# A two-layer decoder kernel: 68 products that nobody reads ahead of blocks of feed-forward products, and a new order

## The chip, the cores and the metric

One Trainium2 chip, one core of it. A time is the device time of one execution of the whole program in microseconds (us); a kernel's time is the median of its timed executions. The engines of the core run side by side, each through its own instructions in order: TensorE (PE) for matrix products, VectorE (DVE) and ScalarE (ACT) for elementwise work, GpSimd (POOL), and SyncE (SP), which issues the loads and stores (DMA).

## The reference

A decoder trunk of two layers on 256 positions of 1024 channels. Layer 0 is a gated linear recurrence and a SwiGLU feed-forward stage; then one key/value projection is made of its output; layer 1 is causal attention over these keys and a second feed-forward stage; a norm ends it. Each stage is modulated by the conditioning vector `c`.

```python
def swiglu(h, w_gate, w_up, w_down):
    return (jax.nn.silu(h @ w_gate) * (h @ w_up)) @ w_down

    for l in range(DEPTH):
        if l == N_A_LAYERS:
            kv_mod = cs @ kv_mod_w + kv_mod_b
            kv = shared_kv(x, kv_mod[:, :D], kv_mod[:, D:], kv_norm, w_kv)
        ...
        h = modulate(rmsnorm(x, norm_mix[l]), sh_m, sc_m)
        ...
        x = x + g_m[:, None, :] * mix
        h = modulate(rmsnorm(x, norm_ffn[l]), sh_f, sc_f)
        x = x + g_f[:, None, :] * swiglu(h, ffn_w_gate[l], ffn_w_up[l], ffn_w_down[l])
    return rmsnorm(x, final_norm)
```

`D_FF` is 2816, all data are float32.

## The kernel before

The stream of activations is kept transposed, as eight tiles of 128 channels by 256 positions. Weights come from memory in units of 128 partitions by up to 2048 columns (`raw_`, loaded by SP). ACT rounds each unit to the fp32r format (`whi_`, line 439), DVE takes the rest (`wlo_`, line 440), and one float32 product is made of three fp32r products (`mm3`, lines 387 to 389): high weights by high activations, high by low, low by high. Each is 128x128 weights by 256 columns. Some products are made in plain fp32 instead (line 449 and the sums of squares); such a product shows as two records.

The two feed-forward stages are f0 and f1 (the function `ffn`). In each, `f_st` are sums of squares over channels (products with a matrix of ones), `f_g` the products of the first 256 hidden channels with the activations not yet normed (`f_u`), so that they can start ahead of the norm, `f_p` those of the others (blocks i = 1 to 10, gate and up, q = 0 and 1), and `f_d` the products back to 1024 channels, eight of two halves with eleven weight tiles each. Behind f0 come the sums `n_st`, the keys `kp` (again with activations not yet normed, `kv_u`), the relative positions `rp` and the values `vp`; the attention ends in `ao`, with the weights `wo`. The residuals (line 611) give the next stream (`f0x`, `x3`), ACT squares it (`n_sq`, `f_sq`) and DVE adds the squares (line 539). The columns of modulation (`sc_`, `sh_`, `g_`) are made on DVE from rows loaded by DMA (line 462).

No loop of the chip sets the order. The program is recorded as operations with a cost in microseconds, reads and writes, and a planner in Python lays them out for each engine: of the operations that are ready, the one of the smallest rank goes first, where the rank is the place in the program plus a number from the table `PRIO`, by engine and kind of tile. Tiles are taken from pools of slots (four of `whi`, four of `wlo`, four of `raw`, eight of PSUM, among others), so an operation that writes a slot waits for the last reader of what lay there.

## Time and profile before

| what | us |
|---|---|
| median of two timed executions | 614.14 (612.71 to 615.57) |
| the profiled execution | 608.61 |
| its span, first to last instruction | 606.8 |
| PE busy in it | 585.9 |
| DVE busy | 471.8 |
| ACT busy | 340.6 |

A row of the profile's timeline is one instruction or a run of like ones on one engine: its start, how long it took, its engine, its line of the kernel, what it writes and reads. PE's products are pipelined: a duration reaches into the next product, so what a product costs is read from one start to the next. In brackets stands how long the engine idled ahead of it and what it waited for.

### The profile page before, as it was taken

Reading aid. Unit: us, or ns where it says so; the run is one execution under the profiler, and the core shown is the slowest. Engines: PE = TensorE matmul, PEld = TensorE weight load, DVE = VectorE, ACT = ScalarE, POOL = GpSimd, SP = SyncE. Lnnn points to the kernel's source line nnn. Section 1 sums busy time; section 2 is a strip of 40 time slices with the busy share of each in tenths; the row PEclk is TensorE's granted clock in tenths of the full one; section 3 lists DMA queues with packets and bytes.
Section 4 is the critical chain, followed back from the end, with each engine's and each line's share of the span. In section 5 each row is a group of like instructions: output and inputs, shape, how many; then the busy total and the mean of one; then the engine's idle time right before and its main releaser. Section 6 shows DMA issues by size and latency. Waiting matters only on the chain.

```text
span 606.8 us, 11423 instructions
## 1 busy us (share of the span) xinstructions
PE 585.9 (97%) x4706; PEld 563.2 (93%) x4706; DVE 471.8 (78%) x743; ACT 340.6 (56%) x509; POOL 1.2 (0%) x10
## 2 busy tenths in 40 slices
PE   3999989999999999999999999998999999999996
PEld 1999868998999999999999889998999999999996
DVE  6998788977997898788878969889997654545542
ACT  6537898718653443343336899747664444434432
POOL 0000000000000000000000000000000000000000
...
GB/s 307 353 339 239 332 355 355 278 383 224 350 312 323 336 348 323 257 334 315 377 295 357 203 143 322 282 332 245 218 306 274 214 203 165 144 144 192 191 1 70
DMA packets 33362, 162.94 MB, mean 269 GB/s; under 512 B 3700, under 2 KB 4893, under 8 KB 23966
## 3 DMA queue, kind: packets, MB, share of 16 engines
...
## 4 chain that ended last, share of the span: by engine, by line
PE 63%; DMA 18%; DVE 12%; ACT 3%; issue 3%; SPq 0%; DVEq 0%; ACTq 0%
PE ps_f_p L388 11%; PE ps_f_p L387 11%; PE ps_f_p L389 11%; PE ps_f_d L388 3%; PE ps_f_d L389 3%; PE ps_f_d L387 3%; PE ps_ga L449 3%; DMA mraw_mr_sh_kv_m__2730<-in_kvmod 2%; DVE wlo_f0c_l L440 2%; DMA raw_sh_f_r<-in_modp 1%; DMA mraw_mr_g_m_m__3469<-in_mod 1%; DMA raw_wix<-in_win_x 1%; PE ps_qp L389 1%; PE ps_qp L388 1%; PE ps_qp L387 1%
## 5 line engine op out<-in xcount | busy, mean ns | idle before, releaser
L388 PE MATMUL ps_f_p<-t_f_l,whi_f0b_h 128*128 128x256 f32 x320 | 89.7, 280 | 0.0
L387 PE MATMUL ps_f_p<-t_f_h,whi_f0b_h 128*128 128x256 f32 x320 | 89.5, 280 | 0.0
L389 PE MATMUL ps_f_p<-t_f_h,wlo_f0b_l 128*128 128x256 f32 x320 | 89.3, 279 | 0.0
L389 PE MATMUL ps_f_p<-t_f_h,wlo_f1b_l 128*128 128x256 f32 x320 | 88.5, 276 | 0.0
L387 PE MATMUL ps_f_p<-t_f_h,whi_f1b_h 128*128 128x256 f32 x320 | 88.4, 276 | 0.0
L388 PE MATMUL ps_f_p<-t_f_l,whi_f1b_h 128*128 128x256 f32 x320 | 88.4, 276 | 0.0
L388 PEld LDWEIGHTS ps_f_p<-t_f_l,whi_f0b_h 128*128 128x128 f32 x320 | 60.1, 188 | 0.2 <-DVE t_f_l L568 0.2
L387 PEld LDWEIGHTS ps_f_p<-t_f_h,whi_f0b_h 128*128 128x128 f32 x320 | 60.2, 188 | 0.0
L389 PEld LDWEIGHTS ps_f_p<-t_f_h,wlo_f1b_l 128*128 128x128 f32 x320 | 60.1, 188 | 0.1
L388 PEld LDWEIGHTS ps_f_p<-t_f_l,whi_f1b_h 128*128 128x128 f32 x320 | 60.1, 188 | 0.0
L387 PEld LDWEIGHTS ps_f_p<-t_f_h,whi_f1b_h 128*128 128x128 f32 x320 | 60.1, 188 | 0.0
L389 PEld LDWEIGHTS ps_f_p<-t_f_h,wlo_f0b_l 128*128 128x128 f32 x320 | 59.8, 187 | 0.0
L440 DVE TENSOR_TENSOR wlo_f1b_l<-raw_f1b_r,whi_f1b_h 128x2048 fp32r<-128x2048 f32 x20 | 45.6, 2289 | 18.1 <-ACT whi_f1b_h L439 18.1
L439 ACT ACTIVATE whi_f1b_h<-raw_f1b_r 128x2048 fp32r<-128x2048 f32 x20 | 38.2, 1912 | 24.8 <-issue 11.9
L439 ACT ACTIVATE whi_f0b_h<-raw_f0b_r 128x2048 fp32r<-128x2048 f32 x20 | 38.2, 1910 | 21.5 <-issue 19.1
L388 PE MATMUL ps_f_d<-t_f_al,whi_f0c_h 128*128 128x256 f32 x176 | 49.2, 280 | 0.8 <-DVE t_f_al L607 0.8
L389 PE MATMUL ps_f_d<-t_f_ah,wlo_f0c_l 128*128 128x256 f32 x176 | 49.3, 280 | 0.0
L387 PE MATMUL ps_f_d<-t_f_ah,whi_f0c_h 128*128 128x256 f32 x176 | 49.1, 279 | 0.0
L440 DVE TENSOR_TENSOR wlo_f0b_l<-raw_f0b_r,whi_f0b_h 128x2048 fp32r<-128x2048 f32 x20 | 45.6, 2287 | 4.2 <-ACT whi_f0b_h L439 4.1
L389 PE MATMUL ps_f_d<-t_f_ah,wlo_f1c_l 128*128 128x256 f32 x176 | 48.6, 276 | 0.0
L387 PE MATMUL ps_f_d<-t_f_ah,whi_f1c_h 128*128 128x256 f32 x176 | 48.6, 276 | 0.0
L388 PE MATMUL ps_f_d<-t_f_al,whi_f1c_h 128*128 128x256 f32 x176 | 48.6, 276 | 0.0
(469 smaller groups left out, 1661.3 us busy)
## 6 DMA issues: line engine op xcount, KB each, us to landing
...
```

The lines of the kernel that those rows point to most:

```text
L387: nc.tensor.matmul(o, h_, a_, start=start, stop=False, skip_group_check=skip)
L388: nc.tensor.matmul(o, h_, b_, start=False, stop=False, skip_group_check=skip)
L389: nc.tensor.matmul(o, l_, a_, start=False, stop=stop, skip_group_check=skip)
L439: act(n - o, lambda: nc.scalar.activation(hi.ap[:, o:n], raw.ap[:, o:n], AF.Copy), (raw,), (hi,))
L440: tt(n - o, lambda: nc.vector.tensor_sub(lo.ap[:, o:n], raw.ap[:, o:n], hi.f[:, o:n]), (raw, hi), (lo,))
L449: pe(n * 0.0016875 + 0.002, lambda: nc.tensor.matmul(ps.ap[:, c:c + n], lo.ap[:, o:o + w], xh.ap[:, xo:xo + n], start=start, stop=stop, sk ...
```

## The change

Two things. First, ahead of 68 blocks of fp32r products in f0 and f1 one product more is issued. The blocks are the first of each eight in `f_p` with j = 0 (i from 2 to 10, q = 0 and 1) and the first of each eleven in `f_d`. The kinds are taken in turn from a list of 24: eighteen are fp32r with 2 to 512 columns, which read the high weights that the next product reads and the first activations; six are fp32 with 2 to 128 columns, a matrix of ones by the identity. All write one PSUM tile of the stage, `f0_side` or `f1_side`, which nothing reads. A block with such a lead asks for the whole tile of activations in place of one half of it. Second, all numbers in `PRIO` are others, so that all engines' orders change. The results are the same.

```diff
 PRIO = {
     "PE": {
-        "cps": -877, "n_st": -1, "xb": 779, "yb": 1804, "ga": -19, "sh_f_ps": -1801, "sh_f_pt": 1118, "wo": -42,
...
+        "n_st": 1947, "xb": 1797, "yb": -17, "ga": -541, "sh_f_ps": 91, "sh_f_pt": 840, "wo": 1008, "g_m_ps": -28,
...
-        def mm3(cost, out, wh, wl, xh, xl, start, stop, R, Wr, skip=False):
+        def mm3(cost, out, wh, wl, xh, xl, start, stop, R, Wr, skip=False, pre=None):
             def fn():
+                if pre is not None:
+                    pre()
                 o = out()
...
+        ahead = [(1, 2), (1, 34), (1, 64), (1, 98), (1, 130), (1, 160), (1, 194), (1, 226), (1, 250), (1, 258), (1, 260),
+                 (1, 262), (1, 266), (1, 272), (1, 288), (1, 320), (1, 384), (1, 512), (0, 2), (0, 16), (0, 33), (0, 64),
+                 (0, 97), (0, 128)]
+        turn_of = [0]
+        side = {}
+
+        def gemm(out, key, wu, o, xu, start, stop, skip=False, w=P, n=S, cost=0.3275, lead=False):
...
+            pre, R, Wr = None, (hi, lo) + ((xh, xl) if n > S or lead else ((xh, xo), (xl, xo))), ((ps, key),)
+            if lead:
+                two, m = ahead[turn_of[0] % len(ahead)]
+                turn_of[0] += 1
+                d = side["ps"]
+                Wr += ((d, 0),)
+                if two:
+                    pre = lambda: nc.tensor.matmul(d.ap[:, :m], hi.ap[:, o:o + w], xh.ap[:, :m], start=True, stop=True)
+                else:
+                    R += (ident, ones)
+                    pre = lambda: nc.tensor.matmul(d.ap[:, :m], ones.ap, ident.ap[:, :m], start=True, stop=True)
+                cost += max(0.1, m * (0.00046 if two else 0.0017))
...
+            side["ps"] = PS(f"{name}_side")
...
-                                gemm((pq[q], j * S), 0, wq[q], (j * KC + k) * P, hx(h, k), k == 0, k == KC - 1)
+                                gemm((pq[q], j * S), 0, wq[q], (j * KC + k) * P, hx(h, k), k == 0, k == KC - 1,
+                                     lead=(j == 0 and k == 0))
...
-                        gemm((ps, 0), 0, wu, kk * P, hx(aa, k), k == 0, k == FT - 1)
+                        gemm((ps, 0), 0, wu, kk * P, hx(aa, k), k == 0, k == FT - 1, lead=(kk == 0))
```

The lines of the changed kernel are numbered 2 to 20 higher: its `mm3` has lines 389 to 391, the conversions are 441 and 442, the squares' sums 559, the residuals 631, the leads 469 (fp32r) and 472 (fp32).

In the new order of PE a lead stands like this inside f0, here of 272 columns; the block that it opens has the weights `f0b81`:

```order
L389 MATMUL ps_f0_p71_2503<-t2_f0_h2_1732,whi_f0b71_h_2406 128x256
L390 MATMUL ps_f0_p71_2503<-t2_f0_l2_1776,whi_f0b71_h_2406 128x256
L391 MATMUL ps_f0_p71_2503<-t2_f0_h2_1732,wlo_f0b71_l_2431 128x256
L469 MATMUL ps_f0_side_1848<-t2_f0_h0_1664,whi_f0b81_h_2534 128x272
L389 MATMUL ps_f0_p81_2649<-t2_f0_h0_1664,whi_f0b81_h_2534 128x256
L390 MATMUL ps_f0_p81_2649<-t2_f0_l0_1675,whi_f0b81_h_2534 128x256
L391 MATMUL ps_f0_p81_2649<-t2_f0_h0_1664,wlo_f0b81_l_2570 128x256
```

It stands directly ahead of the first product of its block and takes the same weights `whi_f0b81_h`.

PE where f0 ends, before. `f0_d7` is the last block of f0, `kp` the keys, `n2_st` the sums:

```order
L389 MATMUL ps_f0_d7_3652<-t2_f0_ah10_3059,wlo_f0c71_l_3585 128x256
L387 MATMUL ps_kp0_3717<-t1_kv_u1_h_3746,whi_wk0_h_3614 128x258
L388 MATMUL ps_kp0_3717<-t1_kv_u1_l_3006,whi_wk0_h_3614 128x258
...
L389 MATMUL ps_kp2_3735<-t1_kv_u2_h_3749,wlo_wk0_l_3636 128x258
L544 MATMUL ps_n2_st_3806<-t1_n2_sq0_3767,ones_132 128x256
...
L544 MATMUL ps_n2_st_3806<-t1_n2_sq7_3808,ones_132 128x256
L387 MATMUL ps_kp3_3742<-t1_kv_u2_h_3749,whi_wk0_h_3614 128x258
```

and after:

```order
L391 MATMUL ps_f0_d7_3637<-t2_f0_ah10_3075,wlo_f0c71_l_3609 128x256
L564 MATMUL ps_n2_st_3796<-t1_n2_sq0_3765,ones_132 128x256
...
L564 MATMUL ps_n2_st_3796<-t1_n2_sq7_3789,ones_132 128x256
L389 MATMUL ps_kp0_3818<-t1_kv_u0_h_2725,whi_wk0_h_3635 128x258
L390 MATMUL ps_kp0_3818<-t1_kv_u0_l_3806,whi_wk0_h_3635 128x258
```

Key products stood behind the last `f_d` and ahead of the sums, and now the sums come first and all key products behind them.

DVE at the same place, before. `f0x_7` is the residual that the last `f_d` gives, `kv_u1_l` the low part of an input of the keys:

```order
L440 TENSOR_TENSOR wlo_wv0_l_3721<-raw_wv0_r_3612,whi_wv0_h_3700 128x2048
L601 SCALAR_TENSOR_TENSOR t1_kv_u1_l_3006<-t1_f0x_1_3236,sc_kv_m_158,t1_kv_u1_h_3746 128x256
...
L611 SCALAR_TENSOR_TENSOR t1_f0x_7_3765<-ps_f0_d7_3652,g_f0_m_157,t1_x1_7_1580 128x256
L539 TENSOR_TENSOR t1_n2_sq0_3767<-t1_n2_sq0_3767,t1_n2_sq1_3769 128x256
...
L539 TENSOR_TENSOR t1_n2_sq0_3767<-t1_n2_sq0_3767,t1_n2_sq3_3773 128x256
L440 TENSOR_TENSOR wlo_wv4_l_3802<-raw_wv4_r_3644,whi_wv4_h_3777 128x2048
```

and after:

```order
L631 SCALAR_TENSOR_TENSOR t1_f0x_7_3763<-ps_f0_d7_3637,g_f0_m_157,t1_x1_7_1591 128x256
L559 TENSOR_TENSOR t1_n2_sq0_3765<-t1_n2_sq0_3765,t1_n2_sq1_3767 128x256
L482 SCALAR_TENSOR_TENSOR mraw_mr_g_m1_m__3734,g_m1_m_168<-mraw_mr_g_m1_m__3734,csb_130 128x1024
L559 TENSOR_TENSOR t1_n2_sq0_3765<-t1_n2_sq0_3765,t1_n2_sq2_3769 128x256
...
L442 TENSOR_TENSOR wlo_wv0_l_3787<-raw_wv0_r_3679,whi_wv0_h_3727 128x2048
L559 TENSOR_TENSOR t1_n2_sq0_3765<-t1_n2_sq0_3765,t1_n2_sq3_3771 128x256
L442 TENSOR_TENSOR wlo_wv4_l_3794<-raw_wv4_r_3751,whi_wv4_h_3784 128x2048
...
L621 SCALAR_TENSOR_TENSOR t1_kv_u0_l_3806<-t1_f0x_0_3148,sc_kv_m_158,t1_kv_u0_h_2725 128x256
```

The low parts for the keys stood ahead of the last residual, and now they stand behind it, behind all sums of squares, a column of modulation (`g_m1`) and two conversions of weights.

DVE where the attention hands over to f1, before. `x3_` are the residuals of the attention, `f1_u0_l` the first low part for f1's `f_g`:

```order
L539 TENSOR_TENSOR t1_f1_sq0_4806<-t1_f1_sq0_4806,t1_f1_sq2_4825 128x256
L582 TENSOR_TENSOR f1_sl_194<-sh_f1_m_170,f1_sh_193 128x8
...
L539 TENSOR_TENSOR t1_f1_sq0_4806<-t1_f1_sq0_4806,t1_f1_sq3_4832 128x256
...
L601 SCALAR_TENSOR_TENSOR t1_f1_u0_l_4859<-t1_x3_0_4797,sc_f1_m_169,t1_f1_u0_h_4813 128x256
...
L601 SCALAR_TENSOR_TENSOR t1_f1_u1_l_4864<-t1_x3_1_4804,sc_f1_m_169,t1_f1_u1_h_4845 128x256
```

and after:

```order
L631 SCALAR_TENSOR_TENSOR t1_x3_7_4892<-ps_ao3_4638,g_m1_m_168,t1_f0x_7_3763 128x256
...
L559 TENSOR_TENSOR t1_f1_sq0_4839<-t1_f1_sq0_4839,t1_f1_sq3_4894 128x256
L442 TENSOR_TENSOR wlo_f1b11_l_4906<-raw_f1b11_r_4678,whi_f1b11_h_4883 128x2048
L533 TENSOR_TENSOR sh_f1_m_170<-sh_f1_m_170,vec_129 128x8
...
L482 SCALAR_TENSOR_TENSOR mraw_mr_g_f1_m__4815,g_f1_m_191<-mraw_mr_g_f1_m__4815,csb_130 128x1024
L602 TENSOR_TENSOR f1_sl_194<-sh_f1_m_170,f1_sh_193 128x8
L621 SCALAR_TENSOR_TENSOR t1_f1_u0_l_4932<-t1_x3_0_4827,sc_f1_m_169,t1_f1_u0_h_4920 128x256
```

Between the last sum of squares and `f1_u0_l` a conversion of weights (`f1b11`) and a modulation column (`g_f1`) have come in, and the column `sh_f1` is finished later.

## Rows read from the trace of the kernel before

**Rows 1.** The page: busy shares, and one of the costliest groups.
```profile
PE 585.9 (97%) x4706; PEld 563.2 (93%) x4706; DVE 471.8 (78%) x743; ACT 340.6 (56%) x509; POOL 1.2 (0%) x10
...
L388 PE MATMUL ps_f_p<-t_f_l,whi_f0b_h 128*128 128x256 f32 x320 | 89.7, 280 | 0.0
```

**Rows 2.** Waits of PE, the first and the last of seven: us in total, times, longest.
```profile
PE ps_xb L677 <- ACT t_h L563: 4.7, 2, 4.4
...
PE ps_f_d L388 <- DVE t_f_al L607: 0.8, 1, 0.8
```

**Rows 3.** PE's timeline from f0 to the keys.
```profile
330.91 0.39 PE L388 MATMUL ps_kp<-t_kv_u_l,whi_wk_h 128*128 128x258 f32 x1 [0.93 <-DVE t_kv_u_l L601]
```

**Rows 4.** PE's timeline from attention to f1.
```profile
416.02 0.67 PE L544 MATMUL ps_f_st<-t_f_sq,ones 128*128 128x256 f32 x2 [2.10 <-DVE t_f_sq L539]
...
417.96 1.89 PE L544 MATMUL ps_f_st<-t_f_sq,ones 128*128 128x256 f32 x8
```

**Rows 5.** Windows inside f0 and f1: us, then busy us and records by engine, PEclk, DMA.
```profile
160.00:260.00 100.00, 100.00 (x852) 100.00 (x851) 83.35 (x103) 44.69 (x40) 0.00 (x0) 1.00 0.87 317
440.00:560.00 120.00, 120.00 (x1062) 120.00 (x1061) 75.83 (x75) 55.08 (x50) 0.00 (x0) 1.00 0.58 207
```

**Rows 6.** PE's timeline in f1: start us, duration us, what.
```profile
433.52 0.28 PE L389 MATMUL ps_f_p<-t_f_h,wlo_f1b_l 128*128 128x256 f32 x1
...
434.11 0.28 PE L388 MATMUL ps_f_p<-t_f_l,whi_f1b_h 128*128 128x256 f32 x1
...
434.53 0.28 PE L387 MATMUL ps_f_p<-t_f_h,whi_f1b_h 128*128 128x256 f32 x1
...
435.10 0.28 PE L389 MATMUL ps_f_p<-t_f_h,wlo_f1b_l 128*128 128x256 f32 x1
```

**Rows 7.** PE's timeline among the query products, with three transpositions between.
```profile
368.77 0.28 PE L389 MATMUL ps_qp<-t_hq_h,wlo_wq_l 128*128 128x256 f32 x1
368.89 0.49 PE L1057 MATMUL ps_pt<-ident,t_e 128*128 128x128 f32 x3
369.13 0.36 PE L387 MATMUL ps_qp<-t_hq_h,whi_wq_h 128*128 128x256 f32 x1
369.33 0.28 PE L388 MATMUL ps_qp<-t_hq_l,whi_wq_h 128*128 128x256 f32 x1
369.45 0.28 PE L389 MATMUL ps_qp<-t_hq_h,wlo_wq_l 128*128 128x256 f32 x1
...
369.79 0.28 PE L389 MATMUL ps_qp<-t_hq_h,wlo_wq_l 128*128 128x256 f32 x1
```

**Rows 8.** PE's timeline at the end of f1.
```profile
598.76 0.50 PE L1121 MATMUL ps_n_st<-ones,t_n_sq 128*128 128x1 f32 x4
599.12 0.63 PE L1125 MATMUL ps_ty<-ident,t_y 128*128 128x128 f32 x4
```

**Rows 9.** PE's timeline at the first values, 512 columns.
```profile
344.07 0.40 PE L387 MATMUL ps_vp<-whi_wv_h,t_hkv_h 128*128 128x512 f32 x1
344.30 0.39 PE L388 MATMUL ps_vp<-wlo_wv_l,t_hkv_h 128*128 128x512 f32 x1
```

**Rows 10.** DVE's timeline from f0 to the keys.
```profile
330.38 0.87 DVE L601 SCALAR_TENSOR_TENSOR t_kv_u_l<-t_f0x,sc_kv_m,t_kv_u_h 128x256 fp32r<-128x256 f32 x2
331.17 0.47 DVE L611 SCALAR_TENSOR_TENSOR t_f0x<-ps_f_d,g_f_m,t_x 128x256 f32<-128x256 f32 x1
331.56 1.47 DVE L539 TENSOR_TENSOR t_n_sq<-t_n_sq,t_n_sq 128x256 f32<-128x256 f32 x3
332.95 2.28 DVE L440 TENSOR_TENSOR wlo_wv_l<-raw_wv_r,whi_wv_h 128x2048 fp32r<-128x2048 f32 x1
```

**Rows 11.** DVE's timeline ahead of f1.
```profile
408.90 1.22 DVE L462 SCALAR_TENSOR_TENSOR mraw_mr_sh_f_m__4722<-mraw_mr_sh_f_m__4722,csb 128x1024 f32<-128x1024 f32 x1
```

**Rows 12.** PE's timeline at the start.
```profile
14.22 4.63 PE L677 MATMUL ps_xb<-t_h,raw_wix 128*128 128x256 f32 x10 [4.41 <-ACT t_h L563]
```

**Rows 13.** ACT's timeline from f0 to the keys.
```profile
329.83 1.91 ACT L439 ACTIVATE whi_wv_h<-raw_wv_r 128x2048 fp32r<-128x2048 f32 x1
```

More of the change, by code (lines that the diff above doesn't have):

```diff
@@ L277 @@
     "PE": {
-        "cps": -877, "n_st": -1, "xb": 779, "yb": 1804, "ga": -19, "sh_f_ps": -1801, "sh_f_pt": 1118, "wo": -42,
-        "g_m_ps": -799, "g_m_pt": -888, "f_st": 65, "f_g": 1113, "f_p": -3, "f_d": 23, "rp": 3432, "kp": -27, "vp":
-        -23, "sp": -62, "pt": -29, "op": 1946, "ao": -145, "ty": 1267,
+        "n_st": 1947, "xb": 1797, "yb": -17, "ga": -541, "sh_f_ps": 91, "sh_f_pt": 840, "wo": 1008, "g_m_ps": -28,
+        "g_m_pt": 229, "f_st": 518, "f_g": 3215, "f_p": 57, "f_side": 21, "f_d": 455, "rp": -23, "kp": -90, "vp":
@@ L281 @@
+        114, "qp": 2130, "sp": -45, "op": 2820, "ao": 2475, "ty": 3296,
     },
     "ACT": {
[L283 to L286 removed]
@@ L297 @@
-        "fc_l": -490, "fx_": -403, "sh_m_m": 317, "relt": 567, "rr": 3993, "kv_sl": -369, "wk_l": 930, "kv_u_l":
-        -2230, "hkv_l": -1, "hq_l": 2204, "bk": 4008, "tk": -586, "kT": 195, "wv_l": 939, "wq_l": 787, "e": -1582,
-        "mx": 84, "sm": -2722, "ol": -556, "wo__l": 6296, "f_sl": -1045, "fa_l": 438, "f_u_l": -1244, "y_": -211,
-        "rs": -315, "out": 1604,
+        "epst": -1881, "ones": 97, "n_sq": -2026, "n_rstd": -228, "b": -473, "sc": 755, "sh": 879, "wix_l": 124,
+        "n_": 2235, "h_l": -3092, "sp_neg": -313, "sp_ab": -1595, "sp_ln": 956, "sp_e": 263, "sp_d": 2320, "sp_z":
@@ L301 @@
+        "mx": 1004, "sm": 10, "ol": 72, "wo__l": 6055, "f_sl": 1215, "fa_l": 1150, "f_u_l": -969, "rs": -377, "out":
+        947,
     },
     "POOL": {
[L303 removed]
+        "ident": 310, "csr": -809, "xpad": -996,
     },
     "SP": {
[L306 to L307 removed]
@@ L308 @@
-        326, "mr_sc_kv_m_": 452, "mr_sh_kv_m_": -1225, "mr_sc_m_m_": -205, "fc_r": -3000, "mr_sh_m_m_": -409,
-        "oneh": 224, "rows": -204, "G": -40, "wk_r": -125, "mr_g_m_m_": -289, "wq_r": 1251, "mr_sh_f_m_": -136,
-        "wo__r": -57, "out": -1015,
+        "crow": -69, "vec": -221, "mr_sc_": 29, "mr_sh_": -752, "wix": 50, "wga_r": 50, "wiy_r": 1024, "sh_f_r":
+        379, "wout_r": 405, "g_m_r": -629, "mr_sc_f_m_": 488, "fa_r": 4528, "fb_r": -246, "mr_g_f_m_": -328,
+        "mr_sc_kv_m_": 30, "mr_sh_kv_m_": -62, "mr_sc_m_m_": 325, "fc_r": -1244, "mr_sh_m_m_": 527, "oneh": -734,
@@ L311 @@
+        "relt": 255, "rows": -1483, "G": -1439, "wv_r": 679, "mr_g_m_m_": -92, "wq_r": 839, "mr_sh_f_m_": -545,
+        "wo__r": -2817, "out": 41,
     },
@@ L441, in parts @@
             return hi, lo
-        def gemm(out, key, wu, o, xu, start, stop, skip=False, w=P, n=S, cost=0.3275):
+        ahead = [(1, 2), (1, 34), (1, 64), (1, 98), (1, 130), (1, 160), (1, 194), (1, 226), (1, 250), (1, 258), (1, 260),
[4 more added lines that the diff above has]
+        def gemm(out, key, wu, o, xu, start, stop, skip=False, w=P, n=S, cost=0.3275, lead=False):
             ps, c = out
@@ L452, in gemm @@
                 return
+            pre, R, Wr = None, (hi, lo) + ((xh, xl) if n > S or lead else ((xh, xo), (xl, xo))), ((ps, key),)
[10 more added lines that the diff above has]
+                cost += max(0.1, m * (0.00046 if two else 0.0017))
             mm3(cost, lambda: ps.ap[:, c:c + n], lambda: hi.ap[:, o:o + w], lambda: lo.ap[:, o:o + w],
-                lambda: xh.ap[:, xo:xo + n], lambda: xl.ap[:, xo:xo + n], start, stop,
-                (hi, lo) + ((xh, xl) if n > S else ((xh, xo), (xl, xo))), ((ps, key),), skip)
+                lambda: xh.ap[:, xo:xo + n], lambda: xl.ap[:, xo:xo + n], start, stop, R, Wr, skip, pre)
         def mod_col(dst, src, key, **k):
```

27 lines of the change are left out of this document (12 added, 15 removed).

## The prediction

> **What bounds the kernel now.** I read the page first: TensorE (PE) is busy 97% of the span [rows 1], so time is lost where PE idles and where a product takes longer than it must. The waits come next [rows 2]: there are seven, from 4.7 us at the first products down to 0.8 us for `t_f_al` inside f0. Four lie ahead of the feed-forward stages. The other two that the change can touch stand in the timeline: 0.93 us for `t_kv_u_l` where f0 hands over to the keys [rows 3] and 2.10 us for `t_f_sq` where attention hands over to f1 [rows 4].
>
> Then two windows, one inside each feed-forward stage [rows 5]. PE is full in both, yet it gets 852 products done in 100 us in f0 (117.4 ns each) and 1062 in 120 us in f1 (113.0 ns each), with the same instruction, shape and granted clock (1.00 in both). So the stream of 256-column products has two paces. The timeline shows one change of pace [rows 6]: five starts from 433.52 to 434.11 are 118 ns apart, then there is a 0.2 us wait, and the five from 434.53 to 435.10 are 114 ns apart; this pace then holds for some 1450 products to the end of f1. In f0 all of some 1490 products of this shape run at the slower one (three lines of 320 records [rows 1] and three of 176). A pace holds until the stream is broken (by a wait or a foreign product) and is then drawn anew: counting restarts in PE's timeline, about one in five comes out fast. After three transpositions it is fast, three starts in 0.34 us from 369.45 [rows 7]; after the 0.8 us wait inside f0 [rows 2] it is slow as before. What decides the draw I can't see.
>
> **The change part by part: the inserted products.** The blocks that get a lead are 18 of `f_p` and 16 of `f_d` in each stage, 68 in all (not 72): in the order 54 of the fp32r kind and 14 of the fp32 kind. They read what the following product reads anyway, or constants, and write one PSUM slot that nobody else uses in the stage, so no other engine waits for them. As PE is full there, whatever they take is added to the end.
> - fp32r, under 256 columns, 9 per turn of 24: no such product is in the trace. The nearest rows are three 128-column transpositions dropped into a stream [rows 7]: from the product ahead of them to the second behind takes 0.56 us (368.77 to 369.33), against 0.236 without them, so 0.108 us each. Loading weights seems to set this, not columns: even a product of one column spends 0.36 us on four records [rows 8]. I take the full spacing of a product, 0.1156 us (mean of both paces): 9 x 0.1156 = 1.04 us.
> - fp32r, 258 to 512 columns: by columns. 512 columns take 0.233 us from start to start [rows 9], 0.455 ns a column. The five from 258 to 272 have 1318 columns, 0.60 us; those of 288, 320, 384 and 512 have 1504, 0.68 us.
> - So a turn of the 18 costs 2.33 us; three turns 7.0 us.
> - fp32, 2 to 128 columns: each runs as two records, 0.18 us for the pair at one column [rows 8]; a 128-column record takes 0.11 us as above. I take 0.22 us: 14 x 0.22 = 3.1 us.
>
> The sum is 10.1 us. **From below**: if the short ones cost only their columns (1158 a turn at 0.455 ns = 0.53 instead of 1.04 us, and some 0.05 us for an fp32 one), it is 10.1 - 1.5 - 2.4 = 6.2 us. **From above**: an fp32 record of 256 columns takes about 0.22 us, eight in 1.89 us with the tail of the last [rows 4]; two records make a product, so 1.7 ns a column; if fp32r below 256 columns ran at that, the nine would take 2.14 us, 3.3 us more over three turns. And the first product behind the transpositions starts 0.20 us ahead of its follower (369.13 to 369.33) instead of 0.118 [rows 7]; if that came on top for all 68, 5.6 us more. That makes 19 us. I stay with 10.1, since the transpositions are the nearest rows and their price holds that delay already.
>
> The row of one column shows about 0.09 us a record [rows 8]. The Trainium skill, "TensorE: Matmul & The Clock Gate", section "Back-to-back issue gap", gives an isolated product of 1 to 64 columns a floor of about 25 ns, and 128 columns 134 cycles. By that floor the short ones would come near the lower bound, and the sum would be about 6 to 7 us; the rows speak against it, because each of these products brings its own weight load.
>
> **The new table of priorities.** All orders change. I compared them joint by joint with the waits above.
>
> *f0 to keys.* Before, the key products whose inputs were ready stand among the last `f_d` products, and PE idles only 0.93 us [rows 3]; the sums `n_st` come when their inputs have long been there. In the new order all 33 products of the last half block come first, then five `n_st`, then the first key product, which needs `kv_u0_l`. On VectorE (DVE) behind the last `f_d` stand now: the residual, a sum of squares, a modulation column, two more sums with the small `g_m1` add and `wlo_wv0` between, then `wlo_wv4` and only then `kv_u0_l`. By [rows 10] and, for the modulation, [rows 11]: residual and `kv_u_l` 0.4 each, sums 0.33 to 0.46, `wlo` 2.2 (2.28 less what overlaps the next), modulation 1.15 likewise. So `n_st` starts 0.2 + 0.4 + 0.33 + 1.15 + 0.33 + 0.1 + 2.2 + 0.33 = 5.0 us behind the last `f_d`, 5.4 with the hand-overs; `kv_u0_l` is there 2.2 + 0.1 + 0.4 us after the third sum, that is at 8.2 us. PE works 5 x 0.43 = 2.2 us of that and idles 6.0 against 0.9 before: **+5.0 us** (bounds +2, if part of that queue runs while `f_d` still does, and +8, if `g_m1`'s DMAs come late and the sums run at half pace after 5 us of idleness). That last thing is seen at the start: behind a wait of 4.4 us ten fp32 records take 4.63 us there, more than 0.4 us each in place of 0.22 [rows 12].
>
> *Attention to f1.* Before, PE waits 2.1 us for the sums [rows 4], with the hand-over 2.3, and the first `f_g` products follow at once, as DVE had little to do in between. In the new order ACT converts `whi_f1b11` ahead of the square of the fourth block; that needs the slot of the last attention weights, so it starts only with the last `ao`, and takes 1.9 us, like one of its size [rows 13]. On DVE `wlo_f1b11` (2.2 us), two adds and a modulation column of `g_f1` (1.2 us) stand between the sums and `f_u0_l`. So the sums start at 2.9 us, and `f_g` at 1.9 + 0.3 + 0.4 + 2.2 + 0.3 + 1.2 + 0.1 + 0.5 = 7.0 us. PE works 2.2 us of that on five sums: 4.8 idle against 2.3: **+2.5 us** (bounds +1 and +5, as DMA for `g_f1` comes in time or not).
>
> *Inside f0.* Before, `f_d` waits 0.8 us for `t_f_al`, behind a `wlo_f0c` on DVE [rows 2]. In the new order `al10` comes 3 us ahead of its use: **-0.9 us** with the hand-over. *Start and the rest*: the small vector is loaded ahead of the conditioning row and the input, +0.3 us; gates, scan, `wo` and the attention body keep their bounds, the wait for `raw_sh_f_r` too: 0.
>
> **The pace.** 68 breaks draw the pace 68 times. At one in five fast, f0 gains 0.22 x 1488 x 4.4 ns = 1.4 us and f1, which in this profile is all fast, loses 0.78 x 1450 x 4.4 ns = 5.0 us: **+3.6 us** against this execution. The bounds are -6.5 (all fast) and +6.4 (all slow).
>
> **The sum**: 608.6 + 10.1 + 5.0 + 2.5 - 0.9 + 0.3 + 3.6 = 629.2 us. The profiled execution is 5.5 us below the median of 614.1, which is what one stage at the slow pace would cost. If the median executions run both stages slow, the drawing gains 0.22 x 12.9 = 2.8 us against them: 614.1 + 16.9 - 2.8 = 628.2 us. Both ways meet near **629 us**, 2.4% above the median.
>
> **The rivals.**
> - *Fast pace for good.* If a foreign product ahead of each block puts the stream into the fast pace, not one time in five but always, f0 loses the 6.5 us too much that it has now: 608.6 + 16.9 - 6.5 = 619 us, and 612 where the joints cost nothing. It decides as soon as more than some two thirds of the draws are fast (629 less 0.45 x 12.9 = 623). For it: the long fast stretch begins right after a break [rows 6]. Against it: f0's own break, the wait for `t_f_al` [rows 2], left the pace slow. It ends within 2%, not slower. Chance 0.16.
> - *Cheap inserts or cheap joints.* The short products cost only columns (-3.9), and DVE works off its queue ahead of the joints (-4.5): 629 - 8 = 621 us; with fast draws as well, below 610. For it: DVE is 76 to 83% busy in these stages [rows 5], so it may run ahead. Against it: the rows of the order behind the last `f_d` all depend on it or stand behind what does. Chance 0.14.
> - *Dear inserts.* The delay behind a foreign product or the price per column of fp32 holds, or a joint's DMA is late and PE drops to half pace: 629 + 7 to 11 = 636 to 640 us. For it: 0.20 us rows [rows 7], half pace at the start [rows 12]. Chance 0.20.
> - *The change doesn't do what it says*: 68 leads, not 72, stand in the order, and that is in the sum already.
>
> **How the numbers follow.** A measurement of this kernel can tell about 2% (12 us) from no change: below 602 is faster, above 626.4 slower. The forecast (0.50) spans 624 to 634, a quarter of it under 626.4: 0.37 slower and 0.13 within 2%. The first rival adds 0.16 within, the second 0.11 within and 0.03 faster, the dear inserts 0.19 slower and 0.01 within. Faster 0.03, within 2% 0.41, slower 0.56. The range is 615 to 640: it takes in most of both cheap cases and nearly all of the dear one.
>
> **What the profile after would show.** Inserts: per block the gap from the product ahead to the second behind grows by about 0.11 us, by 0.23 for 512 columns, and PE is never named as waiting there; a cost near 0.03 or 0.3 proves me wrong. Joints: PE waits near 3 to 5 us ahead of `n_st` and near 3 ahead of the first `kp`, near 2 to 3 ahead of `f_st` and of the first `f_g`. Pace: windows inside f0 and f1 show products per us between 1/0.118 and 1/0.113, with both in one stage, changing at leads. Wrong I would be most through the pace (a kind of lead that always draws fast) or the joints, whose sum rests on the order alone.

## The result, and the profile after

| what | before | after |
|---|---|---|
| median of the timed executions, us | 614.14 | 635.49 (634.80 and 636.18) |
| the profiled execution, us | 608.61 | 634.80 |
| its span, us | 606.8 | 633.0 |

The change made the kernel slower: the ratio of the times is 1.0396, with the interval 1.031 to 1.0482. Forecast were 629.0 us in a range from 615 to 640. (The ratios below are formed without executions that were disturbed, so a ratio need not be the quotient of the medians beside it.)

The page of the kernel after, two of its lines, against [rows 1]: PE is busy 18.3 us longer and idle 7.9 us longer (28.8 against 20.9), and the clock dips past the middle of the span and once again later.

```profile
PE 604.2 (95%) x4788; PEld 580.3 (92%) x4788; DVE 473.6 (75%) x743; ACT 341.6 (54%) x509; POOL 1.2 (0%) x10
PEclk9999999999999999999997999998999999999999
```

The waits of PE after, against [rows 2] (engine, output, line, what it waited for; then total us, times, longest):

```profile
PE ps_n_st L564 <- DVE t_n_sq L559: 8.1, 2, 5.7
...
PE ps_f_st L564 <- DVE t_f_sq L559: 3.5, 1, 3.5
...
PE ps_ao L390 <- DVE t_ol L1099: 2.7, 1, 2.7
```

The 5.7 us ahead of the keys' sums, the 3.5 ahead of f1's sums and the 2.7 inside the attention's `ao` are new or longer; the wait for `t_f_al` inside f0 is gone. No lead is named anywhere.

**The leads.** PE's timeline after, around an fp32r lead of 64 columns, one of 512, and an fp32 lead of 33:

```profile
167.42 0.28 PE L391 MATMUL ps_f_p<-t_f_h,wlo_f0b_l 128*128 128x256 f32 x1
167.54 0.19 PE L469 MATMUL ps_f_side<-t_f_h,whi_f0b_h 128*128 128x64 f32 x1
167.57 0.36 PE L389 MATMUL ps_f_p<-t_f_h,whi_f0b_h 128*128 128x256 f32 x1
167.77 0.28 PE L390 MATMUL ps_f_p<-t_f_l,whi_f0b_h 128*128 128x256 f32 x1
...
253.13 0.40 PE L469 MATMUL ps_f_side<-t_f_h,whi_f0b_h 128*128 128x512 f32 x1
253.36 0.28 PE L389 MATMUL ps_f_p<-t_f_h,whi_f0b_h 128*128 128x256 f32 x1
...
506.64 0.28 PE L391 MATMUL ps_f_p<-t_f_h,wlo_f1b_l 128*128 128x256 f32 x1
506.76 0.30 PE L472 MATMUL ps_f_side<-ident,ones 128*128 128x33 f32 x2
506.90 0.36 PE L389 MATMUL ps_f_p<-t_f_h,whi_f1b_h 128*128 128x256 f32 x1
507.10 0.28 PE L390 MATMUL ps_f_p<-t_f_l,whi_f1b_h 128*128 128x256 f32 x1
507.21 0.28 PE L391 MATMUL ps_f_p<-t_f_h,wlo_f1b_l 128*128 128x256 f32 x1
```

The product behind the short lead starts 0.03 us after it, but the one behind that comes 0.20 us later instead of 0.118: the lead gives at once what its follower then loses, as the transpositions did [rows 7]. From the product ahead of the lead to the second behind, 167.42 to 167.77, are 0.35 us in place of 0.236, so 0.11 us net. Worked out that way for all 68, an fp32r lead costs 0.11 to 0.12 us up to 250 columns and 0.23 to 0.24 at 512, an fp32 one 0.22; together 6.9 + 3.1 = 10.0 us. Behind the fp32 lead the products are 0.11 us apart, ahead of it they were 0.11 to 0.12; the pace comes up again below.

The Trainium skill ("TensorE: Matmul & The Clock Gate", section "Back-to-back issue gap") gives a product of 1 to 64 columns a floor of about 25 ns from start to start. The 30 ns from 167.54 to 167.57 agree with it, but the price is not that gap: the measured 0.11 us decides, and the sum that the prediction estimated by the floor (6 to 7 us) would have been too low.

**The joint behind f0.** Windows of PE after (stretch, length, busy time with its count, granted clock, DMA share, GB/s):

```profile
329.70:335.60 5.90, 0.26 (x3) 0.94 1.00 419
335.60:339.70 4.10, 4.01 (x10) 0.50 1.00 360
339.70:346.00 6.30, 6.30 (x46) 0.84 0.53 197
```

The last `f_d` product starts at 329.69; PE's timeline behind it:

```profile
335.69 4.64 PE L564 MATMUL ps_n_st<-t_n_sq,ones 128*128 128x256 f32 x10 [5.73 <-DVE t_n_sq L559]
339.77 0.78 PE L389 MATMUL ps_kp<-t_kv_u_h,whi_wk_h 128*128 128x258 f32 x1
...
341.20 0.42 PE L391 MATMUL ps_kp<-t_kv_u_h,wlo_wk_l 128*128 128x258 f32 x1
341.42 0.42 PE L389 MATMUL ps_kp<-t_kv_u_h,whi_wk_h 128*128 128x258 f32 x1
```

After 5.7 us of idleness the sums run at a granted clock of 0.50, that is 1.2 GHz in place of 2.4: ten records in 4.1 us instead of 2.2. The first key products follow at that clock too: the first gap is 0.57 us, the next five are 0.22 instead of 0.118 (seven starts, 339.77 to 341.42, in 1.65 us). DVE's timeline in the same stretch:

```profile
329.58 1.23 DVE L482 SCALAR_TENSOR_TENSOR mraw_mr_g_m_m__3714<-mraw_mr_g_m_m__3714,csb 128x1024 f32<-128x1024 f32 x1 [1.00 <-DMA mraw_mr_g_m_m__3714<-in_mod]
...
330.73 0.48 DVE L631 SCALAR_TENSOR_TENSOR t_f0x<-ps_f_d,g_f_m,t_x 128x256 f32<-128x256 f32 x1
...
331.46 1.22 DVE L482 SCALAR_TENSOR_TENSOR mraw_mr_g_m_m__3734<-mraw_mr_g_m_m__3734,csb 128x1024 f32<-128x1024 f32 x1
...
333.02 2.29 DVE L442 TENSOR_TENSOR wlo_wv_l<-raw_wv_r,whi_wv_h 128x2048 fp32r<-128x2048 f32 x1
...
335.55 2.29 DVE L442 TENSOR_TENSOR wlo_wv_l<-raw_wv_r,whi_wv_h 128x2048 fp32r<-128x2048 f32 x1
```

This is the forecast queue, with one thing more ahead of it: another column of modulation had waited 1.00 us for its row, and the last residual stands behind it, 1.04 us after the last `f_d`.

**The attention.** DVE's timeline ahead of `ao`:

```profile
413.02 1.23 DVE L482 SCALAR_TENSOR_TENSOR mraw_mr_sh_f_m__4709<-mraw_mr_sh_f_m__4709,csb 128x1024 f32<-128x1024 f32 x1 [2.70 <-DMA mraw_mr_sh_f_m__4709<-in_mod]
...
414.17 1.42 DVE L1099 TENSOR_TENSOR t_ol<-ps_op,t_oh 128x256 fp32r<-128x256 f32 x4
```

And PE's first `ao` product that needs this `t_ol`:

```profile
414.65 0.39 PE L390 MATMUL ps_ao<-t_ol,whi_wo_h 128*128 128x256 f32 x1 [2.69 <-DVE t_ol L1099]
```

Again a column that waits 2.70 us for its DMA stands on DVE ahead of what PE needs.

**Where the time went.** Stages by PE's timeline, in us; f0 runs from its first `f_g` to its last `f_d`, the others from the last product of one kind to the first of the next, f1 from the last `ao` to the last `f_d`:

| kernel | to f0 | f0 | f0 to `n_st` | f0 to `kp` | f0 to `vp` | `vp` to last `ao` | `ao` to `f_g` | `ao` to end of f1 | span |
|---|---|---|---|---|---|---|---|---|---|
| before | 135.1 | 194.4 | 3.8 | - | 14.5 | 69.6 | 2.7 | 185.0 | 606.8 |
| after | 134.4 | 195.3 | 6.0 | 10.1 | 23.6 | 72.5 | 7.1 | 199.0 | 633.0 |
| e1 | 135.2 | 191.1 | 8.6 | 12.7 | 26.0 | 71.0 | 7.8 | 195.9 | 627.4 |
| e2 | 135.1 | 198.3 | 2.7 | - | 13.3 | 69.9 | 2.2 | 194.7 | 619.6 |
| e5 | 136.7 | 193.8 | 10.5 | 14.5 | 27.1 | 73.7 | 7.8 | 196.9 | 636.4 |
| e6 | 135.5 | 195.5 | 3.0 | 5.1 | 28.6 | 74.5 | 7.0 | 199.0 | 641.3 |
| e7 | 136.2 | 195.3 | 8.1 | 12.0 | 24.7 | 69.9 | 9.7 | 201.0 | 635.2 |
| e10 | 132.2 | 195.4 | 2.6 | 6.3 | 26.3 | 73.3 | 6.8 | 199.0 | 634.4 |
| e11 | 133.6 | 189.4 | 4.3 | 8.4 | 26.9 | 71.1 | 7.5 | 195.1 | 624.3 |

Each row is one execution. Four of them have the order of after at the end of f0 (after, e1, e5, e7), and there the first `vp` comes 23.6 to 27.1 us behind f0, so a difference of two or three us between two rows need not come from the kernels. The traced execution of before is also an early one: 5.5 us below its median and below each of its timed executions on record (610.7 us and more). So the terms read from the traces add up to 26.2 us, where the medians differ by 21.4.

Twelve key products (1.4 us) lie inside f0 before, so f0 alone grew by 0.9 + 1.4 = 2.3 us, and f0 to `vp` by 9.1 - 1.4 = 7.7. Spacing tells the pace: windows of PE after, the stretches of [rows 5]:

```profile
160.00:260.00 100.00, 100.00 (x850) 1.00 0.85 318
440.00:560.00 120.00, 120.00 (x1025) 1.00 0.48 173
```

In the 120 us of f1 stand 1025 records, 25 of them those of 19 leads; that leaves 1000 products of the block, where before it were 1062.

### The profile page after: what moved, and what is told of

Same layout as the page of the kernel before. It is cut to its first block, busy times and chain, and to the rows that moved or that the text cites. A ratio compares the mean times of both kernels' runs of the same rounds, so it can differ in the third digit from the quotient of the medians.

```text
span 633.0 us, 11598 instructions
## 1 busy us (share of the span) xinstructions
PE 604.2 (95%) x4788; PEld 580.3 (92%) x4788; DVE 473.6 (75%) x743; ACT 341.6 (54%) x509; POOL 1.2 (0%) x10
## 4 chain that ended last, share of the span: by engine, by line
PE 82%; DMA 9%; DVE 5%; ACT 2%; issue 1%; SPq 0%; DVEq 0%; ACTq 0%
PE ps_f_p L389 12%; PE ps_f_p L390 12%; PE ps_f_p L391 12%; PE ps_f_d L389 6%; PE ps_f_d L391 6%; PE ps_f_d L390 6%; DMA raw_wix<-in_win_x 3%; PE ps_ga L458 3%; PE ps_f_g L458 2%; PE ps_wo L391 2%; PE ps_wo L390 1%; PE ps_wo L389 1%; DMA raw_wv_r<-in_wv 1%; DMA raw_sh_f_r<-in_modp 1%; DMA mraw_mr_sh_f_m__4709<-in_mod 1%; PE ps_yb L389 1%
## 5 line engine op out<-in xcount | busy, mean ns | idle before, releaser
L389 PE MATMUL ps_f_p<-t_f_h,whi_f1b_h 128*128 128x256 f32 x320 | 90.0, 281 | 0.0
L441 ACT ACTIVATE whi_f1b_h<-raw_f1b_r 128x2048 fp32r<-128x2048 f32 x20 | 38.2, 1912 | 34.1 <-issue 19.7
```

Of the source, the lines that this page charges most:

```text
L389: nc.tensor.matmul(o, h_, a_, start=start, stop=False, skip_group_check=skip)
L441: act(n - o, lambda: nc.scalar.activation(hi.ap[:, o:n], raw.ap[:, o:n], AF.Copy), (raw,), (hi,))
```

## The experiments

**e1: the order alone.** The kernel after with its plan, but no lead issued.

```diff
             def fn():
-                if pre is not None:
-                    pre()
                 o = out()
```

> The changed kernel with its whole plan, but the 68 leads are not issued. Theory (the order alone costs more than the leads): the records of the leads add up to 10.0 us, so 635.5 - 10.0 = 625 us, and up to 2 us more, since the fast stretches that stand behind fp32 leads go; 619 if f1 is drawn fast as a whole. Rival (the leads cost more than their records show, and the order is nearly free): 612 to 617 us.

Measured: 628.94 us, ratio 1.0163 (1.006 to 1.0267). Windows of PE:

```profile
160.00:260.00 100.00, 100.00 (x851) 1.00 0.87 319
440.00:560.00 120.00, 120.00 (x1016) 1.00 0.50 177
```

Without a single lead the whole of both stages runs at the slow pace, f1 too; the joints are as after, with up to 8.4 us ahead of `n_st`. By medians 628.94 - 614.05 = 14.9 us belong to the order, and 635.49 - 628.94 = 6.6 to the leads; the interval of the ratio leaves 3.7 to 16.4 us for the order, so the split is rough.

**e2: the leads alone.** The kernel before with its order; 68 leads of the same 24 kinds in turn, written to the bank that the block itself opens (the two of one `f_d` both ahead of its first half).

```diff
+        def lead_p(*a):
+            turn_of[0] += 1
+            return [ahead[(turn_of[0] - 1) % len(ahead)]]
+
+        def lead_d(l, m, half):
+            return lead_p() + lead_p() if half == 0 else None
...
+                    for two, m in lead:
+                        if two:
+                            nc.tensor.matmul(ps.ap[:, :m], hi.ap[:, o:o + w], xh.ap[:, :m], start=True, stop=True)
+                        else:
+                            nc.tensor.matmul(ps.ap[:, :m], ones.ap, ident.ap[:, :m], start=True, stop=True)
```

> The kernel before with its order on every engine, and the same 68 leads in turn, written into the PSUM of the block that follows; in the products back to 1024 channels the two leads of a block stand together ahead of its first half. Theory: 10 us for the leads, and both stages slow but for the stretches behind the fp32 leads of 16 columns and more: 614.1 + 10 less up to 2 us, so 622 to 625 us. Rival (the leads are nearly free and the new order makes the whole difference): 614 to 617 us.

Measured: 623.01 us, ratio 1.0123 (1.0038 to 1.0207), so 9.0 us for the leads by medians (2.3 to 12.7 by the interval). f0 is 3.9 us longer than before and f1 9.7, and no joint is. The spans of the profiled executions grow by 20.6 (e1) and 12.8 us (e2), 33.4 in all, but by 26.2 in the kernel after: each of the two alone already loses most of before's fast f1, which can be lost only once. The pace behind the leads is as expected in most places, but not in all: it is slow behind all four pairs of fp32 leads, and fast behind one pair of fp32r leads (250 and 258 columns, from 563.28).

**e3: few leads of one kind.** The kernel before with two fp32 leads of 64 columns in each stage, to see whether they turn the pace.

```diff
+        def lead_p(l, i, q):
+            return [(0, 64)] if i == 2 and q == 0 else None
+
+        def lead_d(l, m, half):
+            return [(0, 64)] if m == 1 and half == 0 else None
...
```

> The kernel before with its order, and four fp32 leads of 64 columns only: ahead of the block i = 2 of the products to the hidden channels and ahead of the second block back, in each stage. Theory (an fp32 lead of 16 columns or more starts the fast pace, and it holds until the stream is broken): the products of both stages 113.3 ns apart, 603 to 604 us. Rival (the pace is drawn at random at each break, one in five fast): 609 to 615 us, and no different stretch behind the leads.

Measured: 614.14 us, ratio 0.9994 (0.9948 to 1.004). The first lead does turn f0, as the window of [rows 5] shows: 885 products instead of 852, 3.9 us sooner through `f_p`.

```profile
160.00:260.00 100.00, 100.00 (x885) 1.00 0.86 317
```

In f1 the same lead fails: behind it 988 gaps are slow (117.8 ns), and only the lead in `f_d` brings the fast pace. What f0 gains is all given back in `f_d`. PE's timeline there:

```profile
274.71 0.58 PE L395 MATMUL ps_f_d<-t_f_ah,whi_f0c_h 128*128 128x256 f32 x1 [3.40 <-ACT t_f_ah L622]
276.26 0.58 PE L396 MATMUL ps_f_d<-t_f_al,whi_f0c_h 128*128 128x256 f32 x1 [0.97 <-DVE t_f_al L623]
```

DVE's timeline of e3 ahead of it:

```profile
270.82 1.22 DVE L478 SCALAR_TENSOR_TENSOR mraw_mr_sc_m_m__2976<-mraw_mr_sc_m_m__2976,csb 128x1024 f32<-128x1024 f32 x1 [1.03 <-DMA mraw_mr_sc_m_m__2976<-in_mod]
...
273.31 0.69 DVE L925 TENSOR_TENSOR t_f_f<-ps_f_p,t_f_s 128x512 f32<-128x512 f32 x1
```

`t_f_f`, from which `t_f_ah` and `t_f_al` come, stands on DVE behind columns of modulation that wait for DMA. It starts 134.9 us after the first `f_g`, where before it was 135.1: PE was faster, DVE was not. In the window 277.50 to 281.30 behind the wait the granted clock was 0.50.

**e13: are the columns that cover?** e3, and the columns of modulation that belong to f0's time loaded and multiplied over 64 of 1024 elements (so this kernel computes other modulations).

```diff
+            n = 64 if key[0].name in ("g_f0_m", "sc_kv_m", "sh_kv_m", "sc_m1_m", "sh_m1_m", "g_m1_m") else D
+            load(mr, D, lambda: mr.ap[:, :n], src[:, :n], **k)
...
```

> As e3 (four fp32 leads, the order of before), but the modulation columns that are made during f0 (g_f0, sc_kv, sh_kv, sc_m1, sh_m1, g_m1) load and multiply 64 of their 1024 numbers, so the output differs. Theory (in f0 the loads and VectorE's columns, not PE, set when the last hidden channels are ready, which is why the fast pace there came to nothing in e3): no wait of f_d, and f0 from the first f_g to the last f_d is 187 to 188 us long instead of 194 before and 197 in e3. Rival (the wait has another cause): 192 us or more.

Measured in one execution: 609.72 us. PE has no wait in `f_d` at all, and `f_d` takes 61.8 us against 70.9 in e3 and 64.6 before. But both stretches of `f_p` came out slow, though the leads are e3's, as its windows of PE show for f0, of `f_p` and of `f_d`:

```profile
160.00:260.00 100.00, 100.00 (x852) 1.00 0.53 184
266.50:328.20 61.70, 61.70 (x542) 1.00 0.67 223
```

So f0 took 191.7 us, counted as the 194.4 before and the 196.8 in e3, and lies between the theory's 187 to 188 and the rival's 192, next to the rival's. The last `t_f_f` starts 0.3 us behind the last `f_p` product, where it was 5.3 before at the same slow pace and 9.1 in e3. That the columns and their loads make `t_f_f` late is shown by that, in one execution. That they make the whole wait of e3 is not, since at the slow pace PE came to `f_d` 4.0 us later here; nor that the whole gain of the pace would then arrive.

**e5: all leads alike.** The kernel after with every lead an fp32 product of 64 columns.

```diff
+                two_, m_ = (0, 64)
...
```

> The changed kernel with its plan, all 68 leads fp32 of 64 columns. Theory (they start the fast pace): 5 us more for the leads (15.1 in place of 10.0), 10.5 us less for some 2370 products that become fast: 630 us, faster than the changed kernel by 5. Rival (pace at random, or set by something else): 640 us.

Measured: 632.28 us, ratio 1.026 (1.0184 to 1.0336). Of 53 stretches behind a lead that are long enough to tell, 52 are fast. f0 is 1.5 us shorter than after and f1 2.1, with 5 us more spent in leads, each 0.22 against mostly 0.11. The time is near the theory's 630 and far from the rival's 640, though the intervals of e5 and after overlap.

**e6: the keys first.** The kernel after; a list of moves is applied to its finished plan, so that all else stays: on DVE the two `g_m1` columns, their add, `wlo_wv0` and `wlo_wv4`, and on ACT the conversion of `wv4`, come behind `kv_u3_l`.

```diff
+MOVES = ([1582, 1592, 1596, 1597, 1598, 1602], 1617),
...
```

> The changed kernel with its leads and plan, but where f0 hands over to the keys six instructions are moved behind the low part of the fourth key input: on VectorE the last two modulation columns of g_m1, its add, and the conversions of both value weights; on ScalarE the conversion of the second value weights. Theory (these stand between the last product of f0 and the sums, and the idle time makes the sums run at half pace): PE's wait ahead of the sums falls from 5.7 to 1.5 us, the ten sums take 2.2 instead of 4.1 us: 635.5 - 7 = 628 us. Rival (the weights of keys and values come from memory too late anyway, and PE waits for them a little further on): 634 to 637 us.

Measured: 641.92 us, ratio 1.044 (1.039 to 1.049), slower than after. The wait ahead of `n_st` falls to 2.7 us (1.5 was expected), the sums run at the full clock in 2.1 us, and the first `kp` comes at 5.1 instead of 10.1. What came in its place is the longest of PE's waits:

```profile
PE ps_rp L983 <- DMA relt<-in_relt: 7.6, 1, 7.6
```

Its reason stands on SP's queue, in the timeline of SP:

```profile
328.89 15.07 SPq L406 DMA_DIRECT2D raw_wq_r<-in_wq  x4
344.01 0.42 SPq L406 DMA_DIRECT2D relt<-in_relt  x1
```

The small load of `relt` stands behind four loads of `wq`, as in after. These wait for slots, the longest time (9.7 us) for one that a moved conversion frees, `wlo_wv`; in after, where the conversions come earlier, the four took 12.0 us and PE did not wait for `relt`.

**e10: the small load first as well.** e6, with `relt`'s load ahead of those four.

```diff
+MOVES = ([1582, 1592, 1596, 1597, 1598, 1602], 1617), ([1594, 1600, 1606, 1624], 1643),
...
```

> As e6 (the sums of squares and the first four key inputs ahead of the modulation columns and the conversions of value weights), and on the queue of loads the small table relt goes ahead of the four loads of query weights, behind which rp waited 7.6 us in e6. Theory (the wait of rp only came from loads that stand behind a slot which the moved conversions free later): no wait of rp, the keys begin 5 us behind the last f_d instead of 10, and the whole is 635.5 - 5 to 7 = 629 to 631 us. Rival (the weights behind are too late as well): 634 to 637 us.

Measured: 635.44 us, ratio 1.0319 (1.0228 to 1.041). PE still waits at the same place, now for DVE, as its waits show:

```profile
PE ps_rp L983 <- DVE relt L981: 4.4, 1, 4.4
```

What it waits for is one small instruction that writes eight numbers of `relt`, in DVE's timeline:

```profile
344.37 0.07 DVE L981 MEMSET relt<- 1x8 f32 x1
```

`kp` at 6.3, `vp` at 26.3, later than after's 23.6. DVE has hardly a gap from 334 to 345 us: the columns, the conversions and the low parts of later keys are done there now, and this instruction stands behind them. Behind the wait the key products start 0.21 us apart again until 350.8. By these starts I estimate the loss at 4.4 us of waiting and some 2 us at the lower clock, which is what the moves should have brought. Moving this instruction ahead as well was not tried.

**e11: the same without leads.** e1 with e10's moves.

> As e10, and the 68 leads are not issued. Theory: 628.9 of the run without leads less the same 5 to 7 us, 622 to 624 us, which leaves some 8 us of the order's cost for the attention, f1's start and the pace of f1. Rival: 628 us or more.

Measured: 629.31 us, ratio 1.0193 (1.0136 to 1.0249). No gain over e1's 1.0163, so the rival's time holds. But `rp` waits 3.5 us for the same small instruction here, so the run does not tell whether the amount of DVE's work or the place of this one sets `vp`. Its f0, without leads like that of e1, opens with a fast stretch of 613 products (161.11 to 230.47), where e1's is slow throughout.

**e7: the attention's column.** The kernel after with the column of `sh_f1` behind `t_ol`.

```diff
+MOVES = ([2071], 2084),
...
```

> The changed kernel with its leads and plan, but one modulation column of sh_f1 on VectorE is moved from ahead of the low parts of the attention's output to behind them. Theory (that column waits for its DMA, and the products ao wait 2.7 us behind it): 635.5 - 2.7 = 632.8 us, and no wait of ao. Rival (the column is then late for f1, and the wait comes back ahead of f_st): 635 us.

Measured: 637.27 us, ratio 1.0361 (1.031 to 1.0412). The wait in `ao` is gone and `vp` to the last `ao` is back at 69.9 us; the time comes again at the next joint, among PE's waits:

```profile
PE ps_f_st L589 <- DVE t_f_sq L584: 5.5, 1, 5.5
```

**e8: all joints.** e6 and e7 and, at f1, `f1b11`'s conversions and two columns (`sh_f1`, `g_f1`) moved behind what PE needs.

```diff
+MOVES = ([1582, 1592, 1596, 1597, 1598, 1602], 1617), ([2071], 2084), ([2136], 2147), ([2143], 2148), ([2149, 2157], 2169)
...
```

> Both moves, and at f1 the conversion of f1b11 on both engines and the modulation column of g_f1 go behind the first low part, one column of sh_f1 behind the last sum of squares. Theory (the order's cost lies in three joints): 635.5 - 7 - 2.7 - 2.5 = 623 us, as the old order with leads. Rival (it is spread, or set by DMA): 628 us or more.

Measured: 641.15 us, ratio 1.0427 (1.0384 to 1.0471). PE waits 6.2 us for `relt`, 4.3 ahead of `f_st` and 2.2 at `f_g`.

**e9: leads only where DVE leaves room.** The kernel before with five fp32 leads of 64 columns in f1 alone.

```diff
+        def lead_p(l, i, q):
+            return [(0, 64)] if l == 1 and i in (2, 3, 4) and q == 0 else None
+
+        def lead_d(l, m, half):
+            return [(0, 64)] if l == 1 and m in (0, 1) and half == 0 else None
...
```

> The kernel before with its order, and five fp32 leads of 64 columns in f1 alone (blocks i = 2, 3, 4 of f_p with q = 0, and the first two blocks of f_d). Theory (in f1, where weights are loaded with DMA to spare, the fast pace brings what it should, and most executions of the kernel before run f1 at the slow one): 1.1 us for the leads, 6.2 us less: 609 us. Rival (f1 is already fast in most executions, or another engine sets its length): 614 to 615 us.

Measured: 611.94 us over twelve executions, ratio 0.9942 (0.9906 to 0.9977): 3.4 us faster than before and so faster than both kernels, and less than 2%. In the profiled execution four of the five leads are followed by the fast pace, one by the slow. Nothing ahead of f1 changes there. Its window of PE in f1, where [rows 5] have 1062 records:

```profile
440.00:560.00 120.00, 120.00 (x1056) 1.00 0.59 205
```

So this traced execution (614.83 us) is no faster in f1 than the traced one of before (608.61 us), which was fast there without a lead. The 3.4 us stand between medians; that they come from the pace of f1 is likely, but no trace shows it.

**e12: which kinds turn the pace.** The kernel before with 18 leads in f1, fp32r and fp32 ones in turn.

```diff
+        probe = {(2, 0): (0, 64), (2, 1): (1, 64), (3, 0): (0, 64), (3, 1): (0, 2), (4, 0): (0, 64), (4, 1): (1, 258),
+                 (5, 0): (0, 64), (5, 1): (1, 130), (6, 0): (0, 64), (6, 1): (1, 512), (7, 0): (0, 16), (7, 1): (1, 2),
+                 (8, 0): (0, 128), (8, 1): (1, 250), (9, 0): (0, 33), (9, 1): (1, 320), (10, 0): (0, 97), (10, 1): (0, 2)}
...
```

> The kernel before with its order; in f1 ahead of each of 18 weight blocks of f_p one lead: fp32 ones of 16 to 128 columns, and between them, each behind a stretch that an fp32 lead began, one fp32r lead of 64, 258, 130, 512, 2, 250 or 320 columns or an fp32 one of 2 columns. Theory (the lead's kind sets the pace of the stretch behind it): 113.3 ns behind each fp32 lead of 16 columns or more, 117.8 behind all others. Rival (an fp32r lead leaves the pace as it finds it, and only an fp32 one draws anew): 113.3 ns behind all fp32r leads too.

Measured: 619.24 us in one execution. Behind all seven fp32r leads the pace is slow; three of them broke a fast stretch, as here the one of 258 columns in PE's timeline:

```profile
474.06 0.28 PE L401 MATMUL ps_f_p<-t_f_h,wlo_f1b_l 128*128 128x256 f32 x1
474.18 0.28 PE L399 MATMUL ps_f_p<-t_f_h,whi_f1b_h 128*128 128x256 f32 x1
474.29 0.28 PE L400 MATMUL ps_f_p<-t_f_l,whi_f1b_h 128*128 128x256 f32 x1
...
474.52 0.28 PE L470 MATMUL ps_f_p<-t_f_h,whi_f1b_h 128*128 128x258 f32 x1
...
475.10 0.28 PE L400 MATMUL ps_f_p<-t_f_l,whi_f1b_h 128*128 128x256 f32 x1
475.22 0.28 PE L401 MATMUL ps_f_p<-t_f_h,wlo_f1b_l 128*128 128x256 f32 x1
475.34 0.28 PE L399 MATMUL ps_f_p<-t_f_h,whi_f1b_h 128*128 128x256 f32 x1
```

Behind the fp32 leads it is fast six times (2 columns twice, 64 twice, 128, 97) and slow five times (64 three times, 16, 33). So my rule that an fp32 lead of 16 or more columns always gives the fast pace is wrong, and so is the rival that an fp32r lead leaves the pace as it is.

## Why the prediction was right, and where its sizes were off

| term of the sum, us | predicted | measured |
|---|---|---|
| 68 leads | +10.1 | +10.0 |
| f0 to keys | +5.0 | +7.7 |
| attention, its body | 0 | +2.9 |
| attention to f1 | +2.5 | +2.6 |
| inside f0 | -0.9 | -1.7 |
| start | +0.3 | -0.7 |
| pace | +3.6 | +4.4 |
| not assigned, in f1 | - | +1.0 |
| sum | 20.6 | 26.2 |

The measured terms are after less before in the stage table; the leads are worked out from PE's starts, the pace from the spacing of the products between them (-0.7 in f0, +5.1 in f1). "Inside f0" is what is left of f0's change behind the key products, the leads and the pace. The sums stand against the spans' difference of 26.2 us. The forecast sum of 629.2 lies 5.6 us short of the profiled execution; the keys (+2.7) and the attention (+2.9) make that up, and the other differences cancel.

- **Leads: right.** The price of the transpositions [rows 7] holds for short fp32r products, the price by columns for the long ones, and 0.22 us for fp32. Neither the lower bound nor the dear leads of the third rival came about; the other half of that rival, a late load at a joint and half the pace of PE, did (next point). e1 and e2 put the leads as a whole at 6.6 us on top of the order and 9.0 on top of nothing, by medians and pace included.
- **f0 to keys: mechanism right, size at its upper bound.** PE idled 5.7 us where the sum had 6.0, but the step that PE works "5 x 0.43 = 2.2 us of that" failed: the sums ran at half the clock, 4.1 us (+1.9), and the first key products too (1.65 us for six gaps that take 0.7 at 0.118, +0.9). I had that in the bound "+8", and the row of the start [rows 12] spoke for it. It should have been the value taken, as it came in after, e1, e5, e7, e10 and e11 (`n_st` to `kp` 3.7 to 4.1 us in the stage table), though not in e6 (2.1). The place of the idle time differs as well: all of it is ahead of `n_st`. A modulation column held up the last residual for 1.0 us, and behind the slow sums, at 339.77, `kv_u0_l` had been there for more than a microsecond.
- **Attention: "wo and the attention body keep their bounds" failed.** The new order puts a column that needs a late load ahead of `t_ol` on DVE. I compared the order at the two joints only. e7 removed the wait, and showed that this alone saves nothing: `f_g` then begins 9.7 us behind the last `ao` instead of 7.1.
- **Attention to f1: right in sum, wrong in split.** `f_g` began 7.1 us behind the last `ao` (7.0 forecast); `f_st` began at 3.8 instead of 2.9.
- **Pace: right size for a wrong reason, so by luck.** "Drawn anew" one time in five is not what happens. In the kernel after and the four with its leads and plan (e6, e7, e8, e10) the pattern is the same: of the leads with a stretch behind them that is long enough to tell, all 42 of fp32r and the three fp32 ones of 2 columns are followed by the slow pace, and all eight fp32 ones of 16 or more columns by the fast one, as are 52 of 53 in e5. In the runs with the order of before (e2, e3, e9, e12, e13) fp32 leads of 16 or more columns, pairs among them, are followed by the fast pace only 17 times of 30. There the lead writes the PSUM tile of the block itself and not one of its own, as it does in after and e5; order and tile were changed together, so which of them matters is not shown. Nor do the same instructions always give the same pace: the first lead of e13 leaves f0 slow where that of e3 turns it, and f0 is slow in e1 and begins fast in e11, both without leads. That f1 loses before's fast pace was forecast; but it loses it without leads too (e1), where no lead breaks the stream. What sets the pace at the start of a stage, and why an fp32 lead sometimes fails to turn it, stays open: the first gap behind an fp32 lead was 0.200 to 0.201 us where fast and often, not always, 0.202 to 0.205 where slow.
- **The rival "fast pace for good"** was the nearest to a cure. e5 has the fast pace behind nearly all leads and still takes 632 us, as leads and joints cost more than it brings; e3 and e13 show the other limit, that f0 is bound by DVE and the loads of columns as soon as PE is faster; the 3.4 us of e9, in f1 where that limit is absent, would fit a gain by pace.
- **Two slips in the working** changed no term of the sum: DVE's 75.83 us of 120 in f1 [rows 5] are 63%, not 76, and 1158 columns at 1.7 ns are 2.0 us, not 2.14, which makes the upper bound of the leads 18.5 us, not 19.

**What the joints really cost** was tested four times and came out differently from my theory. I took the queue behind the last `f_d` for an accident of order that moves could undo. e6, e8, e10 and e11 brought the sums forward, and PE then waited for `relt`, for `f_st` and, in e8, for `f_g`'s inputs instead. Windows of all engines (PE, PEld, DVE, ACT, POOL), ahead of and behind the end of f0, in the kernel before:

```profile
270.00:329.60 59.60, 58.82 (x500) 58.62 (x499) 48.98 (x62) 25.68 (x26) 0.00 (x0) 1.00 0.89 332
329.60:344.07 14.47, 13.54 (x100) 12.29 (x98) 13.89 (x27) 11.88 (x25) 0.00 (x0) 1.00 0.59 227
```

and after:

```profile
270.00:329.70 59.70, 59.70 (x516) 59.70 (x514) 43.56 (x52) 23.86 (x20) 0.00 (x0) 1.00 0.84 304
329.70:353.30 23.60, 17.87 (x111) 15.99 (x110) 18.75 (x39) 13.88 (x29) 0.00 (x0) 0.86 0.66 244
```

DVE has 43.56 + 18.75 = 62.3 us of work from 270 us to the first `vp`; before it had 48.98 + 13.89 = 62.9 over about the same work. The new order leaves 18.8 us of it behind f0 in place of 13.9, and e10 leaves 19.7. Inside f0 DVE idles longer in the meantime: 16.1 of the 59.7 us, among them 6.5 for the last product of an `f_d` block (`t_f0x`) and 5.5 for ACT's `whi_f0c`, against 10.6 us before. This speaks for a delay that is made ahead of the joint, while f0 runs, so that what stands where at the joint only chooses who waits. It is argued and not shown: moving DVE's work back into f0 was not tried, and in e10 and e11 the small instruction that held up `rp` stayed where it was.
